# Every second weight unit of the feed-forward part gets its low half from an adding DMA inside SBUF

## The chip, the cores and the metric

One core of one Trainium2 chip runs the whole program. The metric is the device time of one execution in microseconds (us). Engines are named as in the profile: PE is TensorE, DVE VectorE, ACT ScalarE, POOL GpSimd, SP the engine that issues the loads.

## The reference

Two blocks of a network follow each other on 256 tokens of width 2048, all in float32. The first has four kinds of attention, gates and an output product. The second has a product into 4096 columns, four small mixers, an output product, and then the part that matters here:

```
y = rms_norm(h, norm_ffn_g)
h = h + (silu(y @ w_gate) * (y @ w_up)) @ w_down      # w_gate, w_up: 2048 x 5632; w_down: 5632 x 2048
y = rms_norm(h, norm_ple_g)
h = h + sigmoid(y @ w_ple_gate) * (p @ w_ple_proj)    # 2048 x 2048 and 256 x 2048
```

and a last norm. Nearly all work is products of the 256 tokens with weights that are read once.

## The kernel before

The program is a stream of weight units. A unit is 4 row tiles of 128 by 512 columns (1 MB, 8 KB in each of the 128 partitions); a few at the start and for the small products have fewer rows. There are 371 units. Those of the feed-forward part are units 219 to 350 (w_gate and w_up in turn, four units each per 512 columns, and w_down after each group of 4, 4 and 3 column blocks); units 351 to 370 are the last block's gate (four units per 512 columns) and projection (one unit of two row tiles).

Each weight number is split in two numbers of the shorter format float32r, hi and lo with hi + lo = w, and so is the left side. A product is then three matmuls (`product`, lines 217 to 219): left hi times lo, left hi times hi, left lo times hi. A unit has 4 row tiles and 2 token tiles, so 24 matmuls of 128 x 128 by 512 columns; the first of them wants lo.

`run_units` writes out the order by hand. In step s it issues the load of unit s on SP's queue into a tile raw (line 232; 3 buffers), then the split of unit s - 2: ACT copies raw to hi (line 246) and DVE subtracts hi from raw into lo (line 247; 3 buffers of each), then the products of unit s - 4, what follows them when 512 columns are complete (in feed-forward ACT's silu on line 1250, DVE's product on line 1256 or DVE's addition to the residual R on line 1268), and one piece of background work (transposes on PE, line 260, and the split of what they give, lines 276 and 277). Every engine runs its instructions in this order and waits by semaphores for what it reads and for the buffers that it writes. So the split of unit j can begin when PE has finished unit j - 3, whose hi and lo it overwrites, and PE wants it two units later; a load waits until the split three units earlier is done with raw.

POOL is used for few small instructions, such as the power in a norm's scale (lines 266 and 267), and issues some DMAs, of which `to_ffn` has two at the start of the feed-forward part (lines 1226 and 1228).

Of the kernel before, what the change touches and what calls it, by code (L numbers as in the profile page):

```python
# [9 lines left out]
F32 = mybir.dt.float32  # L10
F32R = mybir.dt.float32r
AF = mybir.ActivationFunctionType
ALU = mybir.AluOpType
AX = mybir.AxisListType
PSUM = bass.MemoryType.PSUM
# [17 lines left out]
NHL = 3  # L33
POOL_WINDOWS = (2, 4, 8, 16)
# [6 lines left out]
def shape_constants():  # L41
    """Constants that follow from the shapes alone."""
    u = np.arange(384)
    dist = 255 - u
    d = np.maximum(dist, 0)
    big = np.maximum(d, NBUCKET // 2).astype(np.float32)
    large = NBUCKET // 2 + (
        np.log(big / np.float32(NBUCKET // 2)) / np.float32(math.log(2048 / (NBUCKET // 2))) * np.float32(NBUCKET // 2)
    ).astype(np.int32)
    bucket = np.where(d < NBUCKET // 2, d, np.minimum(large, NBUCKET - 1))  # L50
    oh = np.zeros((P, 384), np.float32)
    for i in range(384):
        if dist[i] >= 0:
            oh[bucket[i], i] = 1.0
    mult = ((d <= 128).astype(int) + ((d % 4 == 0) & (d <= 512)) + ((d % 16 == 0) & (d <= 2048))) * (dist >= 0)
    oh[32] = np.where(dist >= 0, 0.0, NEG)
    oh[33] = np.where(mult > 0, np.log(np.maximum(mult, 1)), NEG)
    sel = np.zeros((2, 12), np.float32)
    sel[0, :8] = 1.0
    sel[1, 8:] = 1.0  # L60
    p = np.arange(P)[:, None]
    j = np.arange(T)[None, :]
    m1 = np.where(p + P - j >= 0, 0.0, NEG)
    mneg = np.concatenate([m1[:, P:], m1], axis=1).astype(np.float32)
    s = np.arange(T)
    upper = (s[:, None] <= s[None, :]).astype(np.float32)
    upper = upper.reshape(2, P, T).transpose(1, 0, 2)
    band = np.zeros((P, 3, 4, P), np.float32)
    for g, w in enumerate(POOL_WINDOWS):
        full = np.zeros((T, T), np.float32)  # L70
        for t in range(T):
            lo = max(0, t - w + 1)
            full[lo : t + 1, t] = np.float32(1.0) / np.float32(min(t + 1, w))
            full[t, t] -= np.float32(1.0)
        band[:, 0, g] = full[:P, :P]
        band[:, 1, g] = full[:P, P:]
        band[:, 2, g] = full[P:, P:]
    ident = np.eye(P, dtype=np.float32)
    return {"c_oh": oh, "c_sel": sel, "c_mneg": mneg, "c_upper": np.ascontiguousarray(upper), "c_band": band, "c_ident": ident}
# [5 lines left out]
)  # fmt: skip  # L85
# [5 lines left out]
def tiled(w):  # L91
    """[k, n] -> [n / 512, k / 512, 128, 4 * 512]: each unit of the weight stream in one piece, a row of it to a partition."""
    k, n = w.shape
    g = min(4, k // P)
    t = w.reshape(k // (g * P), g, P, n // CH, CH).transpose(3, 0, 2, 1, 4)
    return t.reshape(n // CH, k // (g * P), P, g * CH)


def layouts(inputs):
    """The same numbers in other orders: small vectors as columns, x, p and the gating weights transposed, weights in tiles."""  # L100
    cols = np.concatenate([np.asarray(inputs[n]).reshape(-1, P) for n, _ in COLS]).T
    kp = lambda v: v.T.reshape(-1, P, T).transpose(1, 0, 2)
    w = np.asarray(inputs["w_in"])[0]
    small = np.concatenate([w[:, C_IK:C_FOX], w[:, C_FF:C_DIFF]], axis=1)
    main = np.concatenate([w[:, :C_IK], w[:, C_FOX:C_FF], w[:, C_DIFF:]], axis=1)
    out = {"t_" + n: tiled(np.asarray(inputs[n])[0]) for n in TILED}
    out["t_w_in"] = tiled(main)
    out["t_w_branch"] = np.stack([tiled(b) for b in np.asarray(inputs["w_branch"])[0]])
    out["t_small"] = small.reshape(KD, P, NSMALL).transpose(1, 0, 2)
    return {  # L110
        **out,
        "l_cols": cols,
        "l_xT": kp(np.asarray(inputs["x"])[0]),
        "l_pT": kp(np.asarray(inputs["p_2"])[0, 0]),
        "l_sguT": np.asarray(inputs["sgu_w_2"])[0].transpose(2, 0, 1),
    }
# [18 lines left out]
class Unit:  # L135
    def __init__(self, src, nk, ncols, fn):
        self.src, self.nk, self.ncols, self.fn = src, nk, ncols, fn
        self.parts = [nk]  # row tiles that are loaded and split together
        self.beside = lambda k0, k1: None  # runs before a part's load
        self.pre = lambda k0, k1: None  # runs before a part's split  # L140


class Kernel:
# [27 lines left out]
    def need(self, name):  # L171
        """Emit what is left of a named task, and of those before it in its lane."""
        t = self.named[name]
        while not t.done:
            f = t.lane[0]
            f.finish()
            t.lane.remove(f)

# [1 line left out]
    def gemm(self, w, kts, lhs, evac, fresh=None, need=None, sizes=(4,), add=True):  # L180
        """Units for 512 columns of lhs.T @ w; w: their tiles; kts: (row tile of w, tile of lhs), neighbours in a unit.

        fresh() runs before the first unit, need(i) names the task that unit i waits for.
        """
# [36 lines left out]
    def run_units(self):  # L221
        nc, total = self.nc, len(self.units)
        raw, hl = {}, {}
        for s in range(total + NRAW + NHL):
            if s < total:
                u = self.units[s]
                t = self.pw.tile([P, 4 * CH], F32, tag="raw", name="raw", bufs=NRAW)
                v = t[:, : u.nk * u.ncols].rearrange("p (k n) -> p k n", k=u.nk)
                k = 0
                for n in u.parts:  # L230
                    u.beside(k, k + n)
                    nc.sync.dma_start(out=v[:, k : k + n, :], in_=u.src[:, k : k + n, :])
                    k += n
                raw[s] = v
            j = s - (NRAW - 1)
            if 0 <= j < total:
# [4 lines left out]
                vv = v.rearrange("p k n -> p (k n)")  # L241
                k = 0
# [6 lines left out]
                hl[j] = [x[:, :c].rearrange("p (k n) -> p k n", k=u.nk) for x in (hi, lo)]  # L249
# [12 lines left out]
    def rpow(self, out, s, n):  # L262
        """out = (s / n + EPS) ** -0.5"""
# [5 lines left out]
    def split_ps(self, dst, k0, bank, n, scale=None):  # L269
        """bank [P, n * 256] in PSUM -> tiles k0.. of dst (high, low), each tile times scale(k) [P, 1]."""  # L270
# [15 lines left out]
    def split_sb(self, dst, k0, src, n):  # L286
        """src [P, n, 256] in SBUF -> tiles k0.. of dst."""
# [6 lines left out]
    def turn(self, src, nblk, k0, dst, scale=None):  # L294
        """Transpose token-major src(m) [P, nblk * 128] into tiles k0.. of dst, two tiles a step."""
# [7 lines left out]
    def turn_plain(self, src, dst):  # L303
        """src [P, 2, 512] token-major -> dst [P, 4, 256]"""
# [12 lines left out]
    # ------------------------------------------------------------------  # L317
    def build(self):
        tc, nc, a = self.tc, self.nc, self.a
        with ExitStack() as es:  # L320
# [14 lines left out]
            # constants  # L335
# [26 lines left out]
    def start(self):  # L362
        """x comes in pieces beside the first units of the weights."""
# [87 lines left out]
    def softmax4(self, q, k, scale, bias0, bias1, op):  # L451
        """L[t, slot, 0:128 | 128:384] = exp(logits - max) of the two query tiles; r[:, tile * 4 + slot] = 1 / sum."""
# [27 lines left out]
    def weigh(self, slots, v, vh, out):  # L480
        """out(m) <- sum over s of L[t, s] v[s]; slots of L, heads vh of v."""
# [25 lines left out]
    def normed(self, b):  # L507
        """Evacuation into branch b of y, with the softmax's division."""
# [12 lines left out]
    def first_block_units(self):  # L521
        nc, a = self.nc, self.a
        def w(c):
            """The tiles of the 512 columns from c of w_in."""
# [30 lines left out]
        # index queries  # L555
# [58 lines left out]
        # z  # L614
# [14 lines left out]
        # gates and branches  # L629
# [46 lines left out]
        # w_out, the block's residual and norm  # L676
# [49 lines left out]
    def square(self, pool, src, j):  # L726
        """stat[:, j] = sum of src ** 2"""
# [3 lines left out]
    def total(self, out, src, n):  # L731
        """stat[:, out : out + n] = sums of the n fours from stat[:, src]"""
# [4 lines left out]
    def to_merge(self):  # L737
        """Attention's memory goes; the sums of the branches come."""
# [9 lines left out]
    def to_out(self):  # L748
        """The branches' memory goes; x comes again for the residual."""
# [9 lines left out]
    def small_unit(self):  # L759
        """Index keys, index weights and forget gates: 84 columns, weights stationary."""  # L760
# [85 lines left out]
    def fox(self):  # L846
# [5 lines left out]
        # log1p(e) = ln(u) + (e - (u - 1)) / u with u = 1 + e rounded  # L852
# [43 lines left out]
    def diff(self):  # L896
        nc, p1, st = self.nc, self.p1, self.st1
        q, k, v = st["diffq"], st["diffk"], st["diff"]
        # lambda of the differential attention, and the constant part of its norm
# [55 lines left out]
    def to_mixers(self):  # L955
# [17 lines left out]
        # keep s <= t  # L973
        nc.gpsimd.affine_select(out=wr, in_=wr, pattern=[[0, 4], [1, P]], compare_op=ALU.is_ge, fill=0.0, base=0, channel_multiplier=-1)

    def second_block_units(self):
# [21 lines left out]
        def gated(key, out, pad, then):  # L998
            """mx[key] times the product, transposed behind pad zeros."""
# [30 lines left out]
        # conformer  # L1030
# [40 lines left out]
        # spatial gating unit  # L1071
# [61 lines left out]
        # short convolution  # L1133
# [29 lines left out]
        # pooling  # L1163
# [30 lines left out]
        # w_out of the mixers  # L1194
# [45 lines left out]
    def ffn_units(self):  # L1240
        nc, a = self.nc, self.a
        kx = [(k, k) for k in range(KD)]
# [53 lines left out]
        # per-layer embedding and the last norm  # L1296
# [31 lines left out]
        # the last columns one token tile after the other, so that the first tile's end lies under the second's products  # L1328
# [39 lines left out]
    def finish(self, m):  # L1368
        """The last norm of a token tile."""
# [41 lines left out]
```

## Time and profile before

| what | us |
|---|---|
| median of 2 runs | 2130.66 (2130.62 and 2130.71) |
| profiled execution, first to last instruction (span) | 2125.2 |
| around the span (median less span) | 5.5 |
| PE busy | 2106.4 (99%) |
| PE weight loads (PEld), beside the matmuls | 1746.1 (82%) |
| DVE busy | 1155.2 (54%) |
| ACT busy | 913.8 (43%) |
| POOL busy | 36.6 (2%) |

The profiled execution has no time of its own beside its span; the runs' times stand for it. Busy time is the union of an engine's instructions. Matmuls are pipelined: one is listed with about 390 ns, though they follow each other faster than that. A column that names a releaser says which instruction ended an engine's idle time.

### The profile page before, as it was taken

Reading aid. Unit: us, or ns where it says so; the run is one execution under the profiler, and the core shown is the slowest. Engines: PE = TensorE matmul, PEld = TensorE weight load, DVE = VectorE, ACT = ScalarE, POOL = GpSimd, SP = SyncE. Lnnn points to the kernel's source line nnn. Section 1 sums busy time; section 2 is a strip of 40 time slices with the busy share of each in tenths; the row PEclk is TensorE's granted clock in tenths of the full one; section 3 lists DMA queues with packets and bytes.
Section 4 is the critical chain, followed back from the end, with each engine's and each line's share of the span. In section 5 each row is a group of like instructions: output and inputs, shape, how many; then the busy total and the mean of one; then the engine's idle time right before and its main releaser. Section 6 shows DMA issues by size and latency. Waiting matters only on the chain.

```text
span 2125.2 us, 22828 instructions
## 1 busy us (share of the span) xinstructions
PE 2106.4 (99%) x9592; PEld 1746.1 (82%) x9592; DVE 1155.2 (54%) x1000; ACT 913.8 (43%) x854; POOL 36.6 (2%) x65
## 2 busy tenths in 40 slices
PE   8999999999999999999999999999999999999998
PEld 6888888888888888888888888888888888888886
DVE  6457556544454554565599554445444454444554
ACT  5444444434344344445454444343333433334543
POOL 1100000000000000000100000000000000000000
PEclk9999999999999999999999999999999999999999
DMA  7744354455555555564645445555555555555453
GB/s 264 259 157 179 127 190 159 167 191 194 185 195 192 185 198 187 190 238 178 238 168 189 171 176 223 188 190 186 198 189 188 190 186 198 191 186 192 175 178 129
DMA packets 59127, 401.68 MB, mean 189 GB/s; under 512 B 6788, under 2 KB 7440, under 8 KB 12304
## 3 DMA queue, kind: packets, MB, share of 16 engines
q1 hardware_dynamic: 56592, 388.69, 50.7%
q0 software_dynamic: 2288, 11.43, 1.7%
q8 instruction: 75, 1.23, 0.2%
q14 instruction: 28, 0.23, 0.0%
q10 hardware_dynamic: 144, 0.11, 0.0%
HBM read 398.08 MB, written 4.47 MB: 189 GB/s over the span
## 4 chain that ended last, share of the span: by engine, by line
PE 98%; DMA 1%; DVE 0%; issue 0%; ACT 0%; SPq 0%; ACTq 0%; POOLq 0%; POOL 0%; DVEq 0%
PE mm L217 31%; PE mm L219 31%; PE mm L218 31%; PE at L260 2%; DMA raw<-in_t_w_in_dram 1%; PE at L467 0%; PE at L809 0%; DVE lo L247 0%; PE at L459 0%; PE at L504 0%; PE at L503 0%; PE at L501 0%; PE at L808 0%; DVE part L396 0%; PE at L882 0%
## 5 line engine op out<-in xcount | busy, mean ns | idle before, releaser
L247 DVE TENSOR_TENSOR lo<-raw,hi 128x2048 fp32r<-128x2048 f32 (+2 forms) x375 | 841.1, 2245 | 759.7 <-ACT hi L246 759.6
L246 ACT CAST hi<-raw 128x2048 fp32r<-128x2048 f32 (+2 forms) x375 | 700.9, 1871 | 726.6 <-PE mm L219 661.1
L217 PE MATMUL mm<-lo,xA 128*128 128x512 f32 x2176 | 855.3, 393 | 6.2 <-DVE lo L247 6.2
L219 PE MATMUL mm<-hi,xA 128*128 128x512 f32 x2176 | 848.8, 390 | 0.0
L218 PE MATMUL mm<-hi,xA 128*128 128x512 f32 x2176 | 848.2, 390 | 0.0
L217 PEld LDWEIGHTS mm<-lo,xA 128*128 128x128 f32 x2176 | 409.5, 188 | 92.0 <-DVE lo L247 7.0
L219 PEld LDWEIGHTS mm<-hi,xA 128*128 128x128 f32 x2176 | 409.2, 188 | 85.9
L218 PEld LDWEIGHTS mm<-hi,xA 128*128 128x128 f32 x2176 | 409.6, 188 | 84.1
L217 PE MATMUL mm<-lo,xB 128*128 128x512 f32 x608 | 240.2, 395 | 0.0
L219 PE MATMUL mm<-hi,xB 128*128 128x512 f32 x608 | 238.3, 392 | 0.0
L218 PE MATMUL mm<-hi,xB 128*128 128x512 f32 x608 | 236.9, 390 | 0.0
L219 PEld LDWEIGHTS mm<-hi,xB 128*128 128x128 f32 x608 | 114.2, 188 | 25.9
L218 PEld LDWEIGHTS mm<-hi,xB 128*128 128x128 f32 x608 | 114.2, 188 | 24.6
L217 PEld LDWEIGHTS mm<-lo,xB 128*128 128x128 f32 x608 | 114.3, 188 | 23.2
L1022 DVE SCALAR_TENSOR_TENSOR tr<-tr,cols 128x256 f32<-128x256 f32 x128 | 52.4, 477 | 0.0
L217 PE MATMUL mm<-lo,yT 128*128 128x512 f32 x128 | 50.6, 396 | 0.0
L219 PE MATMUL mm<-hi,yT 128*128 128x512 f32 x128 | 50.5, 395 | 0.0
L218 PE MATMUL mm<-hi,yT 128*128 128x512 f32 x128 | 50.5, 395 | 0.0
L729 ACT ACTIVATE junk<-R 128x512 f32<-128x512 f32 x32 | 20.2, 632 | 52.4 <-DVE R L1268 14.5
L276 ACT CAST xB<-at 128x512 fp32r<-128x512 f32 x30 | 16.1, 590 | 59.9 <-PE at L260 59.9
L640 ACT ACTIVATE sig<-mm,rs 128x512 f32<-128x512 f32 x32 | 21.9, 690 | 42.2 <-PE mm L219 42.2
L281 ACT ACTIVATE xA<-at,cols 128x256 fp32r<-128x256 f32 x48 | 21.4, 472 | 40.3 <-DVE xA L282 20.9
(262 smaller groups left out, 818.0 us busy)
## 6 DMA issues: line engine op xcount, KB each, us to landing
raw<-in_t_w_in_dram SPq DMA_DIRECT2D x164, 1024.0 KB, 4.8
raw<-in_t_w_gate_dram SPq DMA_DIRECT2D x44, 1024.0 KB, 4.7
raw<-in_t_w_up_dram SPq DMA_DIRECT2D x44, 1024.0 KB, 4.8
raw<-in_t_w_down_dram SPq DMA_DIRECT2D x44, 1024.0 KB, 4.8
raw<-in_t_w_out_dram SPq DMA_DIRECT2D x32, 1024.0 KB, 4.8
raw<-in_t_w_branch_dram SPq DMA_DIRECT2D x16, 1024.0 KB, 4.8
raw<-in_t_w_ple_gate_dram SPq DMA_DIRECT2D x16, 1024.0 KB, 4.8
raw<-in_t_w_in_dram SPq DMA_DIRECT2D x6, 512.0 KB, 7.3
```

Source lines behind the costliest of these rows:

```text
L217: nc.tensor.matmul(ps, xh[:, k, ts], lo, start=first, stop=False)
L218: nc.tensor.matmul(ps, xh[:, k, ts], hi, start=False, stop=False)
L219: nc.tensor.matmul(ps, xl[:, k, ts], hi, start=False, stop=last)
L246: nc.scalar.copy(out=hi[:, o], in_=vv[:, o])
L247: nc.vector.tensor_tensor(out=lo[:, o], in0=vv[:, o], in1=hi[:, o].bitcast(F32), op=ALU.subtract)
L260: self.nc.tensor.transpose(out, in_, self.ident[: in_.shape[0], : in_.shape[0]])
L276: nc.scalar.copy(out=h, in_=bank[:, : n * T])
L281: nc.scalar.activation(out=hi[:, k0 + i, :], in_=b, func=AF.Copy, scale=scale(k0 + i))
L640: nc.scalar.activation(out=s, in_=ps[m], func=AF.Sigmoid, scale=self.r0(m))
L729: self.nc.scalar.activation(out=t, in_=src, func=AF.Square, accum_out=self.stat[:, j : j + 1])
L1022: nc.vector.scalar_tensor_tensor(out=o, in0=i, scalar=s, in1=o, op0=ALU.mult, op1=ALU.add)
```

## The change

Units numbered above ffn_from (8 after the first of feed-forward, so 227) and below total - 8 (363), with an odd number and 4 row tiles, are marked apart. Such a unit is loaded into a tile rawd of its own with 2 buffers, which belongs to the feed-forward memory; the others keep the 3 buffers of raw. Its split runs on ACT and a DMA: ACT writes the negated rounded weights into lo, POOL issues a DMA from rawd to lo inside SBUF that adds (lo becomes rawd - rounded), and ACT copies rawd to hi. DVE has no part in it. Its `parts` are emptied so that the old split is passed over. The diff also takes comments and descriptions out; this is its core:

```diff
+APART = 2
...
 class Unit:
...
+        self.apart = False
...
     def run_units(self):
         nc, total = self.nc, len(self.units)
+        for i, u in enumerate(self.units):
+            u.apart = i % APART == 1 and self.ffn_from < i < total - 8 and (u.nk, u.ncols) == (4, CH)
...
-                t = self.pw.tile([P, 4 * CH], F32, tag="raw", name="raw", bufs=NRAW)
+                if u.apart:
+                    t = self.p5.tile([P, 4 * CH], F32, tag="rawd", name="rawd", bufs=2)
+                else:
+                    t = self.pw.tile([P, 4 * CH], F32, tag="raw", name="raw", bufs=NRAW)
...
+                if u.apart:
+                    nc.scalar.activation(out=lo, in_=vv, func=AF.Copy, scale=-1.0)
+                    nc.gpsimd.dma_start(out=lo, in_=vv, accum_op=ALU.add)
+                    nc.scalar.copy(out=hi, in_=vv)
+                    hl[j] = [x.rearrange("p (k n) -> p k n", k=u.nk) for x in (hi, lo)]
+                    u.parts = []
...
-                hl[j] = [x[:, :c].rearrange("p (k n) -> p k n", k=u.nk) for x in (hi, lo)]
+                if not u.apart:
+                    hl[j] = [x[:, :c].rearrange("p (k n) -> p k n", k=u.nk) for x in (hi, lo)]
...
     def ffn_units(self):
         nc, a = self.nc, self.a
+        self.ffn_from = len(self.units) + 8
```

## Rows read from the trace of the kernel before

**Rows 1.** The page's first part: busy us, share of the span, instructions.
```profile
PE 2106.4 (99%) x9592; PEld 1746.1 (82%) x9592; DVE 1155.2 (54%) x1000; ACT 913.8 (43%) x854; POOL 36.6 (2%) x65
```

**Rows 2.** The page's fourth part: the chain that ended last, by engine.
```profile
PE 98%; DMA 1%; DVE 0%; issue 0%; ACT 0%; SPq 0%; ACTq 0%; POOLq 0%; POOL 0%; DVEq 0%
```

**Rows 3.** Busy time by stretch, and groups by line (busy, mean | idle before), 1250 to 2050.
```profile
core 0: us, PE busy (x) PEld busy (x) DVE busy (x) ACT busy (x) POOL busy (x), PEclk, DMA share, GB/s
1530.00:1740.00 210.00, 210.00 (x943) 173.95 (x943) 98.74 (x57) 81.58 (x54) 0.00 (x0) 1.00 0.53 189
...
L217 PE MATMUL mm<-lo,xA 128*128 128x512 f32 x749 | 292.3, 390 | 0.0
L217 PE MATMUL mm<-lo,xB 128*128 128x512 f32 x397 | 156.7, 395 | 0.0
```

**Rows 4.** ACT's instructions in order of time, 1553 to 1612: start, us, what.
```profile
1554.02 1.91 ACT L246 CAST hi<-raw 128x2048 fp32r<-128x2048 f32 x1 [3.54 <-PE mm L219]
1559.46 1.91 ACT L246 CAST hi<-raw 128x2048 fp32r<-128x2048 f32 x1 [3.53 <-PE mm L219]
1564.90 1.91 ACT L246 CAST hi<-raw 128x2048 fp32r<-128x2048 f32 x1 [3.53 <-PE mm L219]
1569.66 1.37 ACT L1250 ACTIVATE sg<-mm,rs 128x512 f32<-128x512 f32 x2 [2.85 <-PE mm L219]
1570.93 1.90 ACT L246 CAST hi<-raw 128x2048 fp32r<-128x2048 f32 x1
```

**Rows 5.** Groups by line and form, 1250 to 2050: the split.
```profile
L247 DVE TENSOR_TENSOR lo<-raw,hi 128x2048 fp32r<-128x2048 f32 x143 | 327.9, 2293 | 354.2 <-ACT hi L246 354.2
L246 ACT CAST hi<-raw 128x2048 fp32r<-128x2048 f32 x144 | 275.0, 1911 | 350.7 <-PE mm L219 314.4 <-DVE R L1268 28.7 <-issue 7.6
```

**Rows 6.** POOL's instructions in order of time, 912 to 940.
```profile
912.98 0.78 POOL L756 DMA_DIRECT2D xr<-in_x_dram  x1 [548.16 <-DVE xB L277]
913.77 0.57 POOL L757 DMA_DIRECT2D fw<-in_final_norm_w_dram  x1
```

**Rows 7.** Waits of SP's queue: us in total, times, longest.
```profile
SPq L232 <- DVE lo L247: 1870.7, 356, 13.1
```

**Rows 8.** DMA issues: count, KB each, median us from issue to landing.
```profile
raw<-in_t_w_up_dram SPq DMA_DIRECT2D x44, 1024.0 KB, 4.8
xr<-in_x_dram POOLq DMA_DIRECT2D x1, 2048.0 KB, 9.3
fw<-in_final_norm_w_dram POOLq DMA_DIRECT2D x1, 1024.0 KB, 13.5
fg<-in_final_norm_g_dram POOLq DMA_DIRECT2D x1, 1024.0 KB, 4.9
```

**Rows 9.** DMA queues: packets, MB, engines' share; 1525 to 1745, then 912 to 940.
```profile
q1 hardware_dynamic: 5715, 41.71, 53.0%
...
q0 software_dynamic: 416, 3.15, 29.1%
```

**Rows 10.** Stretches at the start: PE busy first, PEclk third from the end.
```profile
28.00:31.00 3.00, 2.98 (x16) 2.46 (x14) 3.00 (x2) 1.27 (x1) 0.00 (x0) 1.00 0.86 320
31.00:33.60 2.60, 0.00 (x0) 0.00 (x0) 2.60 (x3) 0.00 (x0) 0.00 (x0) 1.00 0.32 79
34.20:37.70 3.50, 3.50 (x12) 2.92 (x12) 1.63 (x2) 0.74 (x2) 0.92 (x2) 0.51 0.66 239
37.70:40.00 2.30, 2.30 (x12) 1.86 (x11) 0.00 (x0) 2.30 (x2) 0.00 (x0) 1.00 0.54 217
```

## Prediction

> **What bounds it now.** I read the profile from the whole to the stretch that is changed. The page's first part has TensorE (PE) busy for 99% of the span and VectorE (DVE) for 54% [rows 1]; the chain of work that ended last is PE for 98% [rows 2]. A matmul's own duration says little, since matmuls overlap, so I looked at feed-forward alone: there PE is busy for all of 210 us at granted clock 1.00, with DVE at 98.74 and ScalarE (ACT) at 81.58 us, and no product on lo has idle time before it [rows 3]. The beat is seen on ACT: without other work, two casts of hi start 5.44 us apart [rows 4]. That is PE's time for the 24 products of a weight unit. PE already runs at the higher of its two clock levels without a gap, so a faster split of the weights can give nothing back here. What the change can do to the time is make PE wait for lo.
>
> **The change, part by part.** Before is one profiled execution of 2125.2 us span; the two runs shown are 2130.62 and 2130.71, so 5.5 us lie around it, and I add my sum to 2130.7. Units are numbered as they are listed: 371 in all, feed-forward from 219, so odd ones from 229 to 361 without the two-tile unit 355 are taken apart: 66, one in each pair of units, and a pair lasts 2 x 5.44 = 10.88 us.
>
> *Removed:* 66 subtractions of 2.29 us on DVE [rows 5], 151 us. They are worth 0: DVE stands idle before them waiting for ACT, and PE never waits for them in this stretch [rows 3, 5].
>
> *Added on ACT:* a negated copy into lo, by the cast of the same size 1.91 us [rows 5], 66 times, 126 us. ACT goes from 81.58/210 = 0.39 to 0.39 + 1.91/10.88 = 0.56 of the time. The worst place is a split behind an evacuation, 1.37 + 2 x 1.91 = 5.19 us, still under 5.44 [rows 4, 5]. Cost 0, hidden under PE; without that cover it would be 126 us. The second half, hi, now comes after the negated copy, but PE takes lo first, so it is not what is late.
>
> *Added on POOL:* 66 issues of 0.57 to 0.78 us [rows 6]. POOL is idle in this stretch [rows 3]; behind a waiting issue on its queue stand only later issues and the two instructions of the next norm's scale. Cost 0.
>
> *The queue of loads:* a load of an apart unit waits until the adding DMA four units earlier has landed, where before it waited for DVE's subtraction three units earlier [rows 7], and the next unit's load is behind it on SP's queue. A load lands 4.8 us after issue [rows 8]; from the latest landing without a PE wait there are 2 x 10.88 - 10.88 - 4.8 = 6 us to its split, so late loads are not the cost. But both loads of a pair now start together when an adding DMA lands.
>
> *The adding DMA itself* is the disputed term; the trace has none. First its time from issue to landing. A unit's split begins when PE has ended the unit three before it, and PE wants its lo two units later: 10.88 us, less 1.91 for ACT, leaves 8.97 us. The nearest rows on the same queue: 1 MB in 4.9 us, 2 MB in 9.3, and 3 MB (both DMAs at 913 us, 913.77 + 13.5 - 912.98) in 14.3 [rows 6, 8]. A copy moves its megabyte in and out side by side. An adding DMA has to read the source and the old lo, and write. If all that overlaps, it is the 4.9 and hidden; if the two reads follow each other, it is like 2 MB; if write and reads follow each other, like 3 MB. I take two, because the copy rows show a read and a write going together, and nothing shows a second read for nothing. Then 9.3 against 8.97 is already late.
>
> Second, the engines' time. Loads take 53.0% of the 16 DMA engines, 5.77 us per pair; the POOL queue moved 3.15 MB in 29.1% of 28 us, 2.72 us per MB [rows 9], so two reads cost 5.44 us. Sum 11.21 us against 10.88: more than a pair holds. And there is a hole: a load is 4.8 us from issue to landing of which 2.88 move data, so 1.9 us pass between the landing of an adding DMA and the loads that it lets go, and the next adding DMA is not there yet, as long as PE's wait s is short (its data starts 4.2 - s us after the landing: 1.91 for ACT, 0.1 to issue, 2.2 = 4.9 - 2.72). So a pair lasts 5.77 + 5.44 + 1.9 = 13.1 us, PE waits 2.2 us before each apart unit, and 66 x 2.23 = 147 us: 2278.
>
> Bounds: one movement, 5.77 + 2.72 + 1.9 = 10.4 under 10.88 and landing well before need: 0. Two without the hole: 0.33 x 66 = 22 us. Three: 5.77 + 8.15 = 13.9, and with s near 3.6 the hole shrinks to 0.6: 14.5 us per pair, 3.6 x 66 = 239 us, 2370. A gain is excluded by the gapless PE.
>
> On this the Trainium skill has a rule, in Collectives: The Full Stack, section "The bandwidth ceiling: the fold count and why AG ≠ RS ≠ AR": an adding transfer runs at half the rate of a copy, not because the sum costs anything but because two source reads go through one read ring. No row of before shows such a transfer; by that rule the term is the two reads of my sum, and the time is the 2278.
>
> **Rivals.** *Hidden (not slower).* The adding DMA is as fast as a copy, 4.9 us. For it: one row per partition, no HBM in it, DMA engines about half idle. Against it: the second read. The point from which it decides is a landing within 8.97 us in the full traffic; then PE's beat stays 5.44 and the time is 2131. The Trainium skill's fit in DMA: Bandwidth & Descriptors, section "Anatomy of one DMA — SWDGE (gpsimd) path", about 2.0 us plus bytes over 436 GB/s, would hide it even with two reads (an estimate: 6.8 us); the trace's 2 MB row is over that, 9.3 [rows 8].
>
> *Three movements or worse.* Reads and writes in SBUF take turns: 2370, and if each row of a partition is finished before the next is begun, beyond 2430. For it: source and target lie in the same memory, unlike any load. Against: nothing in these rows.
>
> *The clock falls.* Once in this trace PE did nothing for 2.6 us, and from 0.6 us after that its granted clock was 0.51 for 3.5 us, the lower level of 1.2 GHz, and then 1.00 again [rows 10]. A wait of 2.2 us per pair is near that. One such stretch costs 1.7 us of PE time, but with pairs set by DMA at 13.1 us PE's 10.88 + 1.7 still fits, the wait only gets shorter; so mostly nothing. If the clock stayed low through the stretch, a pair would take 21.8 us: 2850.
>
> *ACT becomes the bound*, if its copies into lo are slower than its casts: it would need 5.44 instead of 1.91 us or more; nothing shows that.
>
> **Numbers.** Two reads, 2278: 0.43, its own range 2200 to 2340 (half the hole to half the way to three). Hidden, or two reads without the hole: 0.28, 2129 to 2173. Three movements: 0.16, up to 2430. Beyond that, with the clock's fall in it: 0.10. ACT: 0.02, some 2200. Faster: 0.01. The range takes all but the last two and a little: 2128 to 2430. About 2% is what can be told from no change here, 43 us: slower 0.43 + 0.16 + 0.10 + 0.02 = 0.71, within 0.28, faster 0.01.
>
> **What would show it.** In the profile after: adding DMAs with about 9 to 11 us from issue to landing; 66 waits of PE's products on lo, some 2 us each, that name that DMA; the engines' DMA share in feed-forward near 0.85; casts on ACT in 13 us pairs; DVE's busy time down by 151 us and ACT's up by 126. Landings near 5 to 8 us and PE at 100% there would say hidden. A share of DMA well below 0.8 with landings beyond 12 us would say that the adding is slow in itself; a granted clock below 1 in feed-forward would say that waits cost more than their length. Wrong in kind would be PE waiting on loads of raw or on ACT.

## Result, and the profile after

The changed kernel takes 2240.93 us (2235.73 to 2246.13, 2 runs) against 2130.66: 1.052 times as long, 95% interval 1.046 to 1.0575. That is 110 us more; 147 were forecast, and the range held it, though a range from 2128 to 2430 holds nearly every case that was thought of. The profiled execution has a span of 2234.0 us, 108.8 more than before. (Its own time is 2235.73, so 1.7 us lie around a span; the 5.5 us given for before compare two executions, and the one that was profiled there was some 4 us quicker than the two timed runs.)

First the page's first part and its slices (each digit a fortieth of the span), beside [rows 1]:

```profile
span 2234.0 us, 23072 instructions
PE 2146.0 (96%) x9592; PEld 1765.4 (79%) x9592; DVE 1004.0 (45%) x934; ACT 1031.8 (46%) x920; POOL 93.8 (4%) x131
...
PE   8999999999999999999999999999899999899988
...
DMA  7744444555555555656454568888888888888863
```

DVE lost the 151 us that were worth nothing, ACT gained 118, and from slice 25 on, in feed-forward, the DMA engines go from 5 to 8 tenths. PE's busy time grew by 40 us and the rest of the span by 69, so the loss has two parts. The adding DMA's own line (line 251 after: duration of the issue on POOL; who waited for it, us and times; us to landing) has the first:

```profile
L251 POOL DMA_DIRECT2D lo<-rawd x66: 852/862/922, 1332.1 to 2164.6; - x66
...
  PEld mm L219: 80.0, 34
  PE mm L219: 68.0, 34
...
DMA to landing us min/median/max: 6.9/9.4/14.2
```

PE, which had no pause here before [rows 3], waited 34 times for an adding DMA, 68.0 us in all: for half of the 66, 2 us each. The second part stands in the clock. The mean over the span went from 0.998 to 0.983; stretches around one pause (PE busy first, PEclk third from the end) show how:

```profile
1612.00:1614.90 2.90, 2.90 (x13) 2.08 (x12) 1.81 (x1) 0.39 (x1) 0.00 (x0) 1.00 0.98 203
1614.90:1617.50 2.60, 0.03 (x1) 0.00 (x0) 0.00 (x0) 2.60 (x2) 0.78 (x1) 1.00 0.60 123
1617.70:1621.10 3.40, 3.40 (x9) 2.64 (x9) 0.00 (x0) 0.51 (x1) 0.00 (x0) 0.50 1.03 193
1621.10:1624.00 2.90, 2.90 (x14) 2.36 (x13) 0.00 (x0) 0.00 (x0) 0.00 (x0) 1.00 1.00 271
```

After a pause of 2.6 us PE ran 3.4 us at 1.2 GHz, 9 matmuls where the next row has 14 in 2.9 us, as after the one pause of before [rows 10]. There are 16 such stretches in the changed part, 61.4 us together, so about 31 us of PE time. All 16 begin inside or up to 1.2 us behind one of the 19 pauses of 2.2 us or more. 68 and 31 are 99 of the 108.8. Where the last 10 lie is told by the same instructions in both traces; here feed-forward's silu, first before, then after (durations in ns, then first and last start in us):

```profile
L1250 ACT ACTIVATE sg<-mm,rs x22: 689/690/694, 1304.2 to 1924.7; 128x512 f32<-128x512 f32 x22
L1265 ACT ACTIVATE sg<-mm,rs x22: 687/690/690, 1308.0 to 2010.5; 128x512 f32<-128x512 f32 x22
```

3.8 us are lost ahead of the first adding DMA (1332.1), so no adding DMA causes them: in that execution the clock was low for 6.83 us at 34 us, where before had 3.41, and for 3.41 us at 242 us, where before had none. Behind that point 105 us are lost. With the matmuls of both traces set side by side, from start to start, 73.6 us of them lie across the 34 pauses (a listed matmul ends some 0.16 us after the next one's usual start, so the waits are longer than the idle time shown), 28.3 us in the stretches of low clock and 3.3 us in the dozen matmuls after a pause.

Now why the adding DMA is late. Beside [rows 8, 9], issues by kind and the queues in 1600 to 1850, 250 us:

```profile
lo<-rawd POOLq DMA_DIRECT2D x66, 1024.0 KB, 9.4
...
q1 hardware_dynamic: 5695, 41.54, 45.2%
q0 software_dynamic: 2827, 20.54, 41.3%
```

Half the bytes take nearly the same engine time: 20.54 MB in 41.3% of 250 us are 5.3 us for an adding DMA of 1.05 MB; 41.54 MB in 45.2% are 2.85 us for a load. A row of 8 KB took 0.63 us (median of the queue's packets) where one of a load takes 0.309: what two reads, one after the other, would take, though no trace shows the reads themselves. Yet alone this is not too late: the quickest landed in 6.9 us, with 8.97 to go. Most of the lateness comes from loads. One adding DMA is issued at 1606.14; this is the chain of waits there, then the queues in 1604.5 to 1610.5:

```profile
1594.23 9.48 DMA lo<-rawd
...
1606.14 11.32 DMA lo<-rawd
```

```profile
q1 hardware_dynamic: 239, 1.83, 86.7%
issues: line engine op xcount, KB each, median us to landing
raw<-in_t_w_gate_dram SPq DMA_DIRECT2D x1, 1024.0 KB, 9.0
lo<-rawd POOLq DMA_DIRECT2D x1, 1024.0 KB, 11.3
```

The landing before it, at 1603.71, let two loads go at once, as forecast. They are on the engines when the adding DMA comes, and for 4.4 us not one packet of its queue (q0) is among theirs. Its first row started 4.9 us after issue; with idle engines that is 1.43 us. Of the 66, 22 had to wait over 4 us for their first row, and all 22 ended later than 8.9 us after issue; 12 others did, of which six began 2.3 to 3.3 us after issue, and six at 1.4 us but with 97 to 157 rows of loads among their own.

Set beside the pauses, issue by issue: 28 of the 34 (60 us) wait for one of these late ones. Three (2.1 us) wait for a landing 8.6 to 8.9 us after issue, where ACT's silu came ahead of the negated copy and left 7.9 us to need. The other three (0.6, 2.4 and 2.8 us) have landings of 6.9 to 8.7 us and come from ACT: at the end of feed-forward and in the last block it had other work ahead of the negated copy. In one of them PE had ended the unit three before at 2101.79, but ACT split what the transposes give first, the adding DMA was issued at 2107.28, and PE stood 2.4 us:

```profile
2104.71 0.47 ACT L295 ACTIVATE xA<-at,cols 128x256 fp32r<-128x256 f32 x1 [0.58 <-DVE xA L296]
2105.08 1.90 ACT L250 ACTIVATE lo<-rawd 128x2048 fp32r<-128x2048 f32 x1
```

### The profile page after: what moved, and what is told of

Read it like the earlier page. It is cut to its first block, busy times and chain, and to the rows that moved or that the text cites. A ratio compares the mean times of both kernels' runs of the same rounds, so it can differ in the third digit from the quotient of the medians.

```text
span 2234.0 us, 23072 instructions
## 1 busy us (share of the span) xinstructions
PE 2146.0 (96%) x9592; PEld 1765.4 (79%) x9592; DVE 1004.0 (45%) x934; ACT 1031.8 (46%) x920; POOL 93.8 (4%) x131
## 4 chain that ended last, share of the span: by engine, by line
PE 82%; DMA 13%; issue 3%; ACT 2%; DVE 0%; SPq 0%; POOL 0%; POOLq 0%; ACTq 0%; DVEq 0%
PE mm L219 26%; PE mm L221 26%; PE mm L220 26%; DMA lo<-rawd 11%; PE at L274 2%; ACT lo L250 1%; DMA raw<-in_t_w_in_dram 1%; DMA rawd<-in_t_w_gate_dram 0%; PE at L481 0%; PE at L823 0%; DMA rawd<-in_t_w_up_dram 0%; DVE lo L260 0%; PE at L473 0%; ACT hi L259 0%; PE at L518 0%
## 5 line engine op out<-in xcount | busy, mean ns | idle before, releaser
L260 DVE TENSOR_TENSOR lo<-raw,hi 128x2048 fp32r<-128x2048 f32 (+2 forms) x309 | 689.9, 2235 | 913.5 <-ACT hi L259 913.3
L219 PE MATMUL mm<-lo,xA 128*128 128x512 f32 x2176 | 865.2, 398 | 47.1 <-DMA lo<-rawd 39.6
L259 ACT CAST hi<-raw 128x2048 fp32r<-128x2048 f32 (+2 forms) x309 | 575.0, 1863 | 548.5 <-PE mm L221 388.0
L221 PE MATMUL mm<-hi,xB 128*128 128x512 f32 x608 | 242.8, 399 | 0.0
L220 PE MATMUL mm<-hi,xB 128*128 128x512 f32 x608 | 241.8, 398 | 0.0
L250 ACT ACTIVATE lo<-rawd 128x2048 fp32r<-128x2048 f32 x66 | 126.2, 1913 | 145.8 <-PE mm L219 145.8
L252 ACT CAST hi<-rawd 128x2048 fp32r<-128x2048 f32 x66 | 124.5, 1886 | 0.0
L251 POOL DMA_DIRECT2D lo<-rawd x66 | 56.9, 863 | 810.0 <-ACT lo L250 786.3
L291 DVE TENSOR_TENSOR xB<-at,xB 128x512 fp32r<-128x512 f32 x30 | 19.3, 686 | 107.2 <-ACT xB L290 107.2
L221 PE MATMUL mm<-hi,yT 128*128 128x512 f32 x128 | 50.5, 395 | 0.0
```

The lines of the kernel that those rows point to most:

```text
L219: nc.tensor.matmul(ps, xh[:, k, ts], lo, start=first, stop=False)
L220: nc.tensor.matmul(ps, xh[:, k, ts], hi, start=False, stop=False)
L221: nc.tensor.matmul(ps, xl[:, k, ts], hi, start=False, stop=last)
L250: nc.scalar.activation(out=lo, in_=vv, func=AF.Copy, scale=-1.0)
L251: nc.gpsimd.dma_start(out=lo, in_=vv, accum_op=ALU.add)
L252: nc.scalar.copy(out=hi, in_=vv)
```

## Experiments

Theory A: the adding DMA is too slow for PE's need. A1: its two reads alone are enough. A2: they put it out of time only where it meets loads. Rivals: B, ACT's second copy or the changed buffers and order; C, the engines are full, so time does not help; D, late loads. All times beside the kernel before on the same chip, 2129.31 us in the first four and 2128.97 in the last four.

**A plain copy.**

```diff
-                    nc.gpsimd.dma_start(out=lo, in_=vv, accum_op=ALU.add)
+                    nc.gpsimd.dma_start(out=lo, in_=vv)
```

> The changed kernel with a plain copy in place of the adding DMA (lo becomes the weights themselves; the addition is left out). Same queue, same sizes, same waits. Theory A (the adding DMA's own length: each 8 KB row took 0.63 us where a copied row takes 0.309, so it lands too late for PE): rows of 0.31 us, landing 5 to 7 us after issue, no wait of PE on lo, clock 1.00 in feed-forward, 2131 to 2140 us. Rival B (the loss comes from ACT's second copy, from rawd's two buffers or from SP's order of loads): all that is still there, so 2200 us or more.

2136.11 us, ratio 1.0032 (1.002 to 1.0044). The DMA's line (as above):

```profile
L251 POOL DMA_DIRECT2D lo<-rawd x66: 527/537/607, 1330.4 to 2062.0; - x66
...
  PE mm L219: 2.1, 1
...
DMA to landing us min/median/max: 4.1/4.3/10.8
```

Only "add" went, and all but 6.8 of the 110 us with it. Rows took 0.33 us, half of the 0.63. One pause is left, late in the stretch. Landing was quicker than expected, and only 1 of the 66 had to wait over 4 us for its first row: as a copy lands at 4.3, the two loads that it lets go are mostly through before the next copy's rows come.

**DVE adds.**

```diff
-                    nc.gpsimd.dma_start(out=lo, in_=vv, accum_op=ALU.add)
+                    nc.vector.tensor_tensor(out=lo, in0=vv, in1=lo.bitcast(F32), op=ALU.add)
```

> The changed kernel, but DVE adds the weights to the negated lo in place of the DMA. Nothing is left out. ACT's extra copies (66 of 1.91 us), rawd and SP's order stay. Theory A: 2131 us within 5, PE without gaps in feed-forward, DVE back near 1155 us busy. Rival B: 2200 us or more.

2129.49 us, ratio 1.0001 (0.9991 to 1.001). DVE is at 1155.4 us, and PE has no gap (columns as in [rows 3]):

```profile
1600.00:1850.00 250.00, 250.00 (x1114) 206.64 (x1113) 118.12 (x67) 136.18 (x84) 0.00 (x0) 1.00 0.50 193
```

ACT's 126 us, rawd and SP's order cost nothing by themselves; B is out. Here lo is done soon after ACT's negated copy, so this run can't show the three pauses above in which a late copy of ACT and the longer DMA add up.

**lo last in apart units.**

```diff
+                if self.units[self.at].apart:
+                    (xh, xl), mm = st["lhs"], nc.tensor.matmul
+                    for i, (_, lk) in enumerate(g):
+                        for m in range(2):
+                            ts = slice(m * P, m * P + P)
+                            mm(st["ps"][m], xh[:, lk, ts], hi[:, i, :], start=gi == 0 and i == 0, stop=False)
+                            mm(st["ps"][m], xl[:, lk, ts], hi[:, i, :], start=False, stop=False)
+                    for i, (_, lk) in enumerate(g):
+                        for m in range(2):
+                            mm(st["ps"][m], xh[:, lk, m * P : m * P + P], lo[:, i, :], start=False, stop=last and i == len(g) - 1)
+                else:
...
+                self.at = q
                 self.units[q].fn(*hl.pop(q))
```

> The changed kernel with PE's order turned in apart units: the 16 products with hi first, the 8 with lo last, so lo is wanted 16 x 0.227 = 3.6 us later. The adding DMAs stay as they are. Theory A (PE loses only by the lateness of lo, up to 3.4 us, and by the low clock after it): the waits all but vanish and with them the low clock, 2131 to 2150 us, with the engines' DMA share rising towards 1. Rival C (the 16 DMA engines are full: loads 5.6 and adding DMA 5.3 us per pair of 10.88, plus a hole of 1.9 after each landing): the later need moves the wait only, pairs stay over 12 us, 2210 us or more.

2154.95 us, ratio 1.012 (1.0103 to 1.0137). 85 of the 110 us are back, with the adding DMAs no quicker (line 263 is the adding DMA; then the queues in 1600 to 1850):

```profile
  PE mm L216: 20.4, 18
...
DMA to landing us min/median/max: 6.9/10.5/14.2
```

```profile
q0 software_dynamic: 3168, 23.07, 47.8%
q1 hardware_dynamic: 6204, 45.19, 47.6%
```

Lateness is what costs. It was a little over the expected range, and the engines show why: 0.96 busy, near the limit that C had in mind. ACT's negated copies now wait for rawd's loads too, 22 times and 127 us in 1300 to 2100, which in the changed kernel none does. At 0.96 little can be left of C's hole.

**Every fourth unit.**

```diff
-APART = 2
+APART = 4
```

> The changed kernel with every fourth unit apart in place of every second: 33 adding DMAs. Theory A: between two of them the loads of four units have 21.8 us, few adding DMAs queue behind loads, most land in 7 to 9 us, waits under 0.5 us each and no low clock: 2131 to 2150 us. Rival B or any fixed price per apart unit (110 us / 66 = 1.67 us): 2186 us.

2189.05 us, ratio 1.0282 (1.0266 to 1.0297). A miss: half the adding DMAs (34, not the 33 expected) cost half the time, with the engines at 0.72 (stretch as above; then the adding DMA's line):

```profile
1600.00:1850.00 250.00, 237.52 (x1047) 193.00 (x1046) 89.73 (x55) 105.79 (x66) 8.60 (x10) 1.00 0.72 221
```

```profile
  PE mm L219: 44.7, 33
...
DMA to landing us min/median/max: 6.9/10.6/13.1
```

So the engines need not be full. 20 of the 34 had their first row over 4 us after issue: they still meet loads, now those that DVE's splits let go. PE waited for 33. The next run tells whether lateness is all of this price.

**Every fourth unit, lo last.** Both edits above.

> Every fourth unit apart, and lo's products last in apart units. With every fourth unit apart alone, adding DMAs ended 8 to 11.6 us after issue and the engines were busy 0.72. With 3.6 us more before lo is wanted, 12.6 us, theory A2 (only lateness is paid) has no waits left: 2128 to 2136 us. A fixed price of an adding DMA apart from lateness would leave half of the 60 us or more: 2155 us.

2129.19 us, ratio 1.0001 (0.9991 to 1.001), and nobody waits for the adding DMA. Its landings:

```profile
DMA to landing us min/median/max: 6.9/7.4/12.6
```

No fixed price, then. And more than was expected: the first adding DMA ended late in both kernels, 10.6 and 11.2 us after issue; where PE waited for it, later ones went on meeting loads (median 10.6), where it did not, they hardly did (7.4). A wait moves PE against the loads and seems to keep the collisions going.

**Shorter loads.** In the other half of the units:

```diff
+                    u.short = self.ffn_from < s < total - 8 and not u.apart and (u.nk, u.ncols) == (4, CH)
+                    m = 1 if u.short else n
+                    nc.sync.dma_start(out=v[:, k : k + m, :], in_=u.src[:, k : k + m, :])
...
+                if u.short:
+                    vb = v[:, 0:1, :].to_broadcast([P, 4, CH])
+                    h3, l3 = [x.rearrange("p (k n) -> p k n", k=4) for x in (hi, lo)]
+                    nc.scalar.copy(out=h3, in_=vb)
+                    nc.vector.tensor_tensor(out=l3, in0=vb, in1=h3.bitcast(F32), op=ALU.subtract)
+                    u.parts = []
```

> The changed kernel, in which the other half of the units in feed-forward loads only one of its four row tiles (256 KB) and splits that one four times; the other three row tiles' weights are left out of the computation. ACT, DVE, PE and the adding DMAs do as much as before. Theory A2 (an adding DMA alone is 6.7 us from issue to its last row and in time for the 8.97; what makes it late is meeting loads on the engines): most adding DMAs land within 9 us, hardly a wait, 2128 to 2150 us. Theory A1 (its own two reads per row are enough to make it late): rows still 0.63 us and waits as before, 2200 us or more.

2141.91 us, ratio 1.0061 (1.0046 to 1.0076). The adding DMA's line:

```profile
L253 POOL DMA_DIRECT2D lo<-rawd x66: 852/862/922, 1332.2 to 2072.5; - x66
...
  PE mm L219: 9.1, 7
...
DMA to landing us min/median/max: 6.9/7.8/11.9
```

66 adding DMAs with 0.63 us rows as before, and 9.1 us of pauses in place of 68.0: A2, not A1. Only 2 had to wait over 4 us for their first row. 6.3 of the 9.1 us stand before the same three units at which ACT comes late in the changed kernel.

**Three rawd buffers.**

```diff
-                    t = self.p5.tile([P, 4 * CH], F32, tag="rawd", name="rawd", bufs=2)
+                    t = self.p5.tile([P, 4 * CH], F32, tag="rawd", name="rawd", bufs=3)
...
-                s = sg[m] = self.p5.tile([P, CH], F32, tag="sg", name="sg", bufs=4)
+                s = sg[m] = self.p5.tile([P, CH], F32, tag="sg", name="sg", bufs=2)
...
-        t = pool.tile([P, CH], F32, tag="junk", name="junk", bufs=2)
+        t = pool.tile([P, CH], F32, tag="junk", name="junk", bufs=1)
```

> The changed kernel with three rawd buffers in place of two (room for it from two sg buffers in place of four and one junk in place of two). A load of an apart unit then waits for the adding DMA six units earlier. Theory D (part of the loss is late loads: raw lands 8 to 10 us after issue and ACT waits 128 us for it): loads are a pair further ahead, ACT's waits for raw go, and the time falls below 2190 us. Theory A2 (the loss is the adding DMA that queues behind loads; a deeper buffer still has its load let go at a landing): the time stays 2215 to 2245 us, and first rows of adding DMAs still come up to 5 us after issue.

2240.22 us, ratio 1.0523 (1.0507 to 1.0539): no change, as A2 had it, with 77.0 us of pauses and 27 of 66 first rows over 4 us after issue. D it leaves half open, since the deeper buffer did not put the loads ahead: ACT's waits before hi grew from 128 to 185.7 us. But in the DVE run ACT has 96.4 us of the same waits and nothing is lost, and the trace of the changed kernel settles it there. All 34 pauses end with an adding DMA, and no negated copy waited for its load: 50 began when PE let them, ten right behind a silu and six behind other work of ACT.

```profile
L250 ACT ACTIVATE lo<-rawd x66: 1895/1912/1923, 1329.9 to 2162.4; 128x2048 fp32r<-128x2048 f32 x66
...
  PE mm L219: 145.8, 50
```

So late loads cost nothing in the changed kernel, and D is out.

**Two halves.**

```diff
-                    nc.gpsimd.dma_start(out=lo, in_=vv, accum_op=ALU.add)
+                    for o in (slice(0, 2 * CH), slice(2 * CH, 4 * CH)):
+                        nc.gpsimd.dma_start(out=lo[:, o], in_=vv[:, o], accum_op=ALU.add)
```

> The changed kernel with each adding DMA issued as two of two row tiles (512 KB, 4 KB rows). PE wants the first half at the old time and the second 12 x 0.227 = 2.7 us later. Theory A2: the first half has half the data, some 2.6 us less, so waits of up to 3.4 us mostly go, and the engines' time stays: between the 2155 of lo last and 2190 us. If the two halves queue behind loads twice, or small rows cost more, no gain: 2230 us or more.

2189.51 us, ratio 1.0285 (1.0269 to 1.03), at the upper end of what was expected: 40.7 us of pauses (34), and 4 stretches of low clock.

None of these beats the kernel before, which fits [rows 3]: PE has no gap there that a faster split could close.

## Why the prediction was right, and where it was not

*That nothing could be won:* right. The 151 us of DVE were taken off and gave nothing; with DVE adding in the DMA's place the time is the same too.

*POOL and the order of loads at 0:* right, by the DVE run and by what ended PE's pauses. *ACT at 0:* nearly. Its own copies fit, but the worst place was not the split behind a silu (5.19 us): in three units ACT's other work made the adding DMA late, 5.7 us of pauses. An issue took 0.86 us on POOL, more than the 0.57 to 0.78 of [rows 6]; it costs only that much delay.

*The adding DMA at the engine time of two reads:* right. 5.44 us per 1024 KB were taken for it, 5.3 were found; a DMA share near 0.85 was forecast, it is 0.87 in 1600 to 1850. The three movements did not happen. The Trainium skill, Collectives: The Full Stack, section "The bandwidth ceiling: the fold count and why AG ≠ RS ≠ AR", states for the rings of collectives that the second read halves the rate; 0.63 us against 0.309 and 0.33 agrees with that here, for a transfer inside SBUF.

*Its landing:* right in the number by luck. 9.3 us were taken from a 2 MB copy that ran beside loads, and by them every adding DMA would be late by itself. Alone it lands in 6.9 us, in time for 8.97. The median of 9.4 mixes such landings with others that stood behind loads, up to 14.2.

*The rival of the Trainium skill's fit*, DMA: Bandwidth & Descriptors, section "Anatomy of one DMA — SWDGE (gpsimd) path", which would have hidden it (6.8 us for the bytes of two reads, an estimate): nearly right for an adding DMA that meets no load, 6.9 at the least, and wrong in the traffic of this kernel.

*The period of 13.1 us:* wrong in its make-up, and the term that was mis-sized. I had PE wait 2.23 us before each of 66 units, from 11.21 us of engine time and a hole of 1.9. PE waited 2 us for 34 of them, 1.03 per unit apart, and with the low clock a pair lasted 12.5 us (10.88 and a 66th of the 105). The engines' sum does not set the time: with lo last they run at 0.96 for 2155 us, and with every fourth unit at 0.72 they still cost 60 us. The hole's effect is that the loads which a landing lets go stand in front of the next adding DMA. I let the two share the engines; the trace has one wait for the other. (The range given for two reads, 2200 to 2340, is also wider than its own working, which gives 2215 for half the hole and 2324 for half the way to three.)

*The clock:* I priced its fall at mostly nothing, since pairs would be set by DMA anyway. With waits at half of the units only, PE does have to make up for it: some 30 of the 110 us. The two errors, 68 in place of 147 and some 30 in place of 0, go against each other, so it is by luck that the forecast is nearer than its working. When a pause brings the clock down stays open: 16 stretches behind 34 pauses here, 2 behind 33 mostly shorter ones with every fourth unit.

## What to carry to other kernels

A transfer that is nearly hidden is judged by its latest landing, not by its engines' share: ask which other transfers its landing lets go and whether they stand in front of the next one. Where something comes late, want it later before making it faster: turning the order of 24 matmuls took back 85 of 110 us and, with half the adding DMAs, all. Pauses of PE cost more than their length when the clock falls after them, here some four tenths as much again.

## Not expected of the hardware

An adding DMA issued behind two loads had no row on the engines for 4.4 us of their traffic, and its first came up to 5.8 us after issue in place of 1.43. Issue alone does not decide it: one issued at 1921.59, 0.2 and 0.6 us ahead of two loads, had its first row at 5.3 us as well. A load's first row comes 0.96 us after issue on free engines, so theirs came first there too (1922.79). Where an adding DMA is further ahead they mix: of two loads issued 0.8 and 1.2 us after the one of 1616.72 the first row came 3.1 us after issue, and from 1618.5 to 1625 both queues move (columns: packets, MB, share):

```profile
q0 software_dynamic: 112, 0.92, 82.1%
q1 hardware_dynamic: 80, 0.66, 24.9%
```

Why the two queues mix in this case and not in the other no run here shows. An issue on POOL of an adding DMA took 0.86 us, of the plain copy 0.54.
